# An encoder block on one core: one hand-written TensorE order, single stores for branch B's tiles, paired weight halves on GpSimd, and gate steps moved ahead of the last transpositions

## The chip, the cores and the metric

The kernel runs on one core of a Trainium2 chip. Inside the core, TensorE multiplies matrices, VectorE and ScalarE work on whole tiles, GpSimd does some of the element-wise work, and SyncE (SP in the profile) issues the transfers between the device's memory and the on-chip memory. [...] TensorE's results land in a memory of their own, PSUM.

The metric is the device time of one execution in microseconds (us).

## The reference

The kernel computes one encoder block on 1024 tokens of width 1024, with 16 learned meta tokens put in front (1040 rows):

```python
h = concatenate([meta_tokens, x])
n = rms_norm(h, norm_mix)
qa, ka, va, qb, kb, vb, ga, gb = split(n @ w_in)
y_a = differential_attention(qa, ka, va)   # 4 heads, all 1040 keys, two softmaxes each
y_b = windowed_gqa(qb, kb, vb, sink)       # 8 heads, 2 key groups, keys within 128 tokens and the meta tokens
merged = sigmoid(ga) * (y_a @ w_branch_a) + sigmoid(gb) * (y_b @ w_branch_b)
h = h + merged @ w_out
h = h + (silu(m @ w_ff_gate) * (m @ w_ff_up)) @ w_ff_down     # m = rms_norm(h, norm_ffn)
out = rms_norm(h, norm_final)[16:]
```

All products are made in float32 quality: each operand is split into a high half and a low half, and TensorE adds three products of halves (high by high, high by low, low by high).

## The kernel before

The work on TensorE has five stretches, one after the other.

**Projections and branch B (to about 295 us).** The normalised tokens lie transposed in `hT_hi` and `hT_lo`. `project_steps` multiplies them by 128 columns of `w_in` at a time; results go through a stage buffer (`qk_stage`, `va_stage`) and out to the device's memory (`qa_d`, `ka_d`, `va_d`; stores at lines 649, 657, 659, 666). Between these products run branch B's tiles: `attend_b(g, t, qb)` does the 4 heads of key group `g` for token tile `t` (scores, softmax, transposition, values), and its `finish` writes the tile's 64 x 512 result with four stores of 64 x 128 into `yb_d` (line 445). There are 16 such tiles. In this stretch the order of the instructions on each engine is set by a planner, which simulates the program with costs of its own.

**Branch A beside the gates (about 295 to 623 us).** For each of 4 heads and 8 token tiles, `scores_a` makes scores and two softmaxes, `transpose_a` turns the result through TensorE, and `values_a` multiplies by the values. The gate products (`ga` and `gb` for the same tokens) fill the gaps. They are done by a seven-product scheme over column pairs `k` and parts `p`: `order_g` lists 56 products, and `gate_steps` gives each as four steps of three matmuls (line 881), so there are 224 steps. The operand of a product is made on GpSimd by `weights_g`: sums of raw weight blocks where the part needs them (lines 780 to 793), a cast for the high half (line 799) and a subtraction for the low half (line 800). Raw weights come with the loads at line 760, at most four ahead.

Head 0's keys and queries are loaded by `load_a` (lines 943 and 945, key half m=1 first), its values by `load_v`, and one quadrant of `hT` is overwritten with mixed tokens by `turn_into(2)` (line 824). All these loads, and branch B's stores, are issued by SP in one line.

The order in this stretch is written out by hand: inside `tc.manual_schedule` an engine keeps program order. For the first token tile the program does two weight operands, `load_a`, two more, `load_v`, then `fill(G_FIRST)`, which is 24 gate steps (six products, 72 matmuls), and `turn_into(2)`. Then the tile's slots run: a character string says in which order one step each of scores (`s`), transposition of the tile before (`t`), gates (`g`) and the tail (`n`, values and norm of earlier tiles) comes. `SLOTS` is used for tiles 0 to 23 and `SLOTS_LAST`, the same string, for 24 to 32, where number 32 only finishes tile 31. A gate step is only given out while `n_gates` lasts: it starts at 224 - `HOLD` = 202, and the last 22 steps come after the loop.

Before the change, this hand-written order is cut in two. The first manual stretch covers TensorE and GpSimd and ends after `turn_into(2)`; a second one, for TensorE alone, begins there. Within each piece the order is kept; how the two pieces mix at the seam is the planner's.

**Merging the branches (623 to 710 us), output projection (to about 804 us), FFN (to the end).** `yb_d` is read back for the merge at line 1142. These stretches are not touched by the change.

Helpers that the rows name: line 120 is the subtraction of `split`, line 926 the copy of far distances for a tile (`far_copy`), line 995 the copy of the meta keys' weights that the third transposition of a tile needs, line 994 the combination of the two softmaxes, lines 980 and 984 the scores' bias and minimum on VectorE, line 887 and line 894 copies of gate results out of PSUM.

Of the kernel before, what the change touches and what calls it, by code (L numbers as in the profile page):

```python
# [9 lines left out]
F32 = mybir.dt.float32  # L10
# [4 lines left out]
ALU = mybir.AluOpType  # L15
# [4 lines left out]
P = 128  # L20
S = 1024
# [5 lines left out]
NT = S // P  # L27
# [11 lines left out]
PP2 = 2  # L39
COMBINE_POOL = (0, 1, 2, 3)  # L40
SLOTS = "ssgsgntssgsgntgnt"
SLOTS_LAST = "ssgsgntssgsgntgnt"
S_BUFS = (2, 2)
AT_BUFS = 2
G_BUFS = 3
# [29 lines left out]
def encoder_block(ctx: ExitStack, tc: tile.TileContext, x, meta, norm_mix, w_in, lq1, lk1, lq2, lk2,  # L75
# [7 lines left out]
    def f32(ap):  # L83
        return ap.bitcast(F32)
# [20 lines left out]
    t_d = [dram.tile([P, 2, 4, 512], F32, name=f"t_d{i}") for i in range(4)]  # L105
    u_d = [dram.tile([P, 512], F32, name=f"u_d{i}") for i in range(8)]
    ya_d = [dram.tile([P, S], F32, name=f"ya_d{h}") for h in range(4)]
    yb_d = [dram.tile([P, S], F32, name=f"yb_d{h}") for h in range(4)]

    ident = const.tile([P, P], F32, name="ident")  # L110
    make_identity(nc, ident)
# [270 lines left out]
    def attend_b(g, t, qb):  # L382
        nm = f"{g}_{t}"
        b0, b1 = max(t - 1, 0), min(t + 2, NT)
        nb = b1 - b0
        W = nb * 144
        j0 = b0 - t + 1
        tb = tbx[:, j0:j0 + nb, :].rearrange("p j k -> p (j k)")
        st = bpool.tile([P, 4, 432], F32, tag="bs", name=f"bs_{nm}", bufs=2)
        mn = small.tile([P, 4], F32, tag="bmn", name=f"bmn_{nm}")  # L390
        dn = small.tile([P, 4], F32, tag="bdn", name=f"bdn_{nm}")
        es = small.tile([P, 4], F32, tag="bes", name=f"bes_{nm}")
        hs = slice(4 * g, 4 * g + 4)
        for r in range(4):
            ps = bank(psum1, "bs", f"bps_{nm}_{r}", 2)
            for v in range(2):
                nc.tensor.matmul(ps[:, :W], qb[:, r, t * P:(t + 1) * P],  # L397
                                 kb[g][:, v, b0:b1, :].rearrange("p b k -> p (b k)"), start=(v == 0), stop=(v == 1))
            nc.vector.tensor_tensor_reduce(st[:, r, :W], ps[:, :W], tb, 2.0 ** -(4 * g + r + 1), nsink[:, 4 * g + r:4 * g + r + 1],  # L399
                                           ALU.add, ALU.min, mn[:, r:r + 1])  # L400
        nc.vector.tensor_tensor(es, mn, sinkb[:, hs], ALU.add)
        for r in range(4):
            nc.scalar.activation(st[:, r, :W], st[:, r, :W], AF.Exp, bias=mn[:, r:r + 1], scale=-1.0,
                                 accum_out=dn[:, r:r + 1])
        nc.scalar.activation(es, es, AF.Exp)
        nc.vector.tensor_tensor(dn, dn, es, ALU.add)
        nc.vector.reciprocal(dn, dn)  # L407
        for r in range(4):
            scaled.append(nc.gpsimd.tensor_scalar(st[:, r, :W], st[:, r, :W], dn[:, r:r + 1], 1.0, ALU.mult, ALU.mult))  # L409

        md = mds[t % 2]
        own = (t - b0) * 144 + P
        nc.gpsimd.tensor_copy(md.rearrange("p (r a k) -> p r a k", r=4, a=2),
                              st[:, :, own:own + NM].unsqueeze(2).broadcast_to([P, 4, 2, NM]))

        def finish():
            py = bank(psum1, "by", f"bpy_{nm}", 1)
            for k in [8, *range(b0, b1)]:
                o = (k - b0) * 144
                pt = bank(psum1, "bt", f"bpt_{nm}_{k}", 2).rearrange("p (r t) -> p r t", r=4)  # L420
                if k == 8:
                    nc.tensor.transpose(pt[:, 0, :], md, ident)
                    tm = tms[t % 2]
                    hi = bpool.tile([P, P], F32R, tag="bmh", name=f"bmh_{nm}", bufs=1)
                    nc.scalar.activation(hi, pt[:, 0, :], AF.Copy, scale=of_hi)
                    for r in range(4):
                        at = slice(32 * r, 32 * r + 32)
                        nc.vector.scalar_tensor_tensor(tm[at, r], pt[at, 0, :], of_x[at], f32(hi[at]), ALU.mult, ALU.subtract)
                    nc.tensor.matmul(py, vb[g][:, 8, :], tm.rearrange("p r t -> p (r t)"), start=True, stop=False)
                    continue  # L430
                for r in range(4):
                    nc.tensor.transpose(pt[:, r, :], st[:, r, o:o + P], ident)
                tr = bpool.tile([P, 2, 4, P], F32R, tag="btr", name=f"btr_{nm}_{k}", bufs=4)
                nc.scalar.activation(tr[:, 0], pt, AF.Copy)
                nc.vector.tensor_tensor(tr[:, 1], pt, f32(tr[:, 0]), ALU.subtract)
                for hl in range(2):
                    nc.tensor.matmul(py, vb[g][:, k, :], tr[:, hl].rearrange("p r t -> p (r t)"),  # L437
                                     start=False, stop=(k == b1 - 1 and hl == 1))
            y1 = bpool.tile([64, 512], F32, tag="by1", name=f"by1_{nm}", bufs=2)
            nc.scalar.copy(y1, py[64:128])  # L440
            nc.vector.tensor_tensor(y1, py[0:64], y1, ALU.add)
            for jj in range(2):
                for par in range(2):
                    r = 2 * jj + par
                    nc.sync.dma_start(yb_d[2 * g + jj][64 * par:64 * par + 64, t * P:(t + 1) * P],
                                      y1[:, r * P:(r + 1) * P])
        return finish

    qb = new_qb(0)
# [309 lines left out]
                    after.enter_context(tc.issue_after(keys_a[0].ins))  # L759
                raws_g.append(nc.sync.dma_start(w, w_in[:, col:col + P].rearrange("(c p) n -> p c n", p=P)))  # L760

    sums_g, keys_a, raws_g, values_in, turned_t = {}, [], [], [], {}

    def weights_g(n):
        k, p = order_g[n]
        load_g()
        tt = nc.gpsimd.tensor_tensor
        nm = f"{k}_{p}"
        kind = "s" if n >= n_first else "m" if p == 6 and k < 5 else "f"
        wa, wb = raw_g[kind, k, 0], raw_g.get((kind, k, 1))  # L770
        a11, a12 = wa[:, 0:4], wa[:, 4:8]
        if wb is not None:
            a21, a22 = wb[:, 0:4], wb[:, 4:8]
        if p == 1:
            src = a11
        elif p == 2:
            src = a12
            n_freed[0] += 1 if k < 5 else 2 if k < 7 else 0
        elif p == 6:
            tt(a21, a21, a22, ALU.add)  # L780
            tt(a21, a21, a11, ALU.subtract)
            src = a21
            if k < 5 or k == 7:
                n_freed[0] += 2
        elif p == 5:
            src = sums_g[k] = gwork.tile([P, 4, P], F32, tag="s", name=f"s1g_{k}", bufs=1)
            tt(src, a21, a22, ALU.add)
        elif p == 7:
            tt(a21, a11, a21, ALU.subtract)
            src = a21  # L790
        elif p == 3:
            tt(a12, a12, a11, ALU.add)
            tt(a12, a12, sums_g.pop(k), ALU.subtract)
            src = a12
        else:
            src = a22
            n_freed[0] += 2
        op = ops_g[n] = wpool.tile([P, 2, 4, P], F32R, tag=("wh", "wl")[n % 2], name=f"wopg_{nm}", bufs=W_BUFS)
        nc.gpsimd.tensor_copy(op[:, 0], src)
        tt(op[:, 1], src, f32(op[:, 0]), ALU.subtract)  # L800

    def ensure_g(n):
        while n_made[0] < min(n, len(order_g)):
# [267 lines left out]
        if t % 4 == 3:  # L1071
            yield from normed_a(h, t // 4, acc[0])

    order_pe = tc.manual_schedule(engines={mybir.EngineType.PE, mybir.EngineType.Pool})
    order_pe.__enter__()
    tiles, turning, tail = [], iter(()), []

    def step_tail():
# [3 lines left out]
    for n in range(AH * NT + T_LAG):  # L1082
# [3 lines left out]
        if n < AH * NT:  # L1086
            h, t = divmod(n, NT)
            if t == 0:
                if not h:
                    ensure_g(2)  # L1090
                ld = load_a(h)
                if not h:
                    ensure_g(4)
                load_v(h, ld[2])
                fill(G_HEAD if h else G_FIRST)
                if not h:
                    turn_into(2)
                    order_pe.__exit__(None, None, None)
                    order_pe = tc.manual_schedule(engines={mybir.EngineType.PE})
                    order_pe.__enter__()  # L1100
            if t % 2 == 0:
                at_ = apool.tile([P, 9, 2, 256], F32R, tag="at", name=f"at{h}_{t}", bufs=AT_BUFS)
            s = [None, None]
            tiles.append((h, t, s, at_, ld[2]))
            scoring = scores_a(h, t, ld, s)
        if n >= T_LAG:
            turning = turn(tiles[n - T_LAG])
        for what in SLOTS if n < 3 * NT else SLOTS_LAST:
            if what == "s":
                next(scoring, None)  # L1110
            elif what == "t":
                next(turning, None)
            elif what == "n":
                step_tail()
            else:
                fill(1)
# [22 lines left out]
        nc.sync.dma_start(raw.rearrange("p (c n) -> p c n", n=P), w_bb[:, o * P:(o + 1) * P].rearrange("(c p) n -> p c n", p=P))  # L1139
    for j in range(4):  # L1140
        for h in range(2):
            nc.sync.dma_start((a12, w11)[h][:, j], yb_d[j][:, h * 512:h * 512 + 512])
    ypool, close_ypool = pool("ypool")
    first_w = [branch_w(ypool, o, w_bb, "b", raw) for o, raw in enumerate((a11[:, 2], asum[:, 0]))]

# [725 lines left out]
```

## Time and profile before

| | us |
|---|---|
| median of 3 runs | 1429.8 (1429.32 to 1431.39) |
| the profiled execution | 1430.58 |
| its span, first to last instruction | 1428.7 |
| TensorE busy in it | 1404.2 (98%) |
| VectorE, ScalarE, GpSimd busy | 917.9, 672.7, 636.9 |

A row of the timeline gives the start in us from the span's start, the duration, the engine, the source line and the operation; in square brackets stands the idle time just before it and what ended that. "SPq" is the time in which SP issues a transfer, not the time of the transfer. Matmuls overlap in the pipeline: one is recorded with 0.39 us, while the next starts 0.23 us later, so the spacing of the starts is what one costs.

### The profile page before, as it was taken

How to read it: one execution, taken by the hardware profiler on the slowest of the kernel's cores; microseconds unless marked ns; L12 is line 12 of the kernel's file. 1: busy time of each engine (PE TensorE's matmuls, PEld its weight loads, DVE VectorE, ACT ScalarE, POOL GpSimd, SP SyncE). 2: the span in 40 equal slices, each digit the busy share in tenths (PEclk: the TensorE clock that was granted, in tenths of full speed). 3: DMA queues.
4: the chain of work that ended last, by engine and by line, in shares of the span. 5: the costliest groups of instructions: out<-in, count | busy, mean ns of one | idle time of the engine just before them, and what ended most of it. 6: DMA issues, size and time to landing. Idle time of an engine off the chain costs nothing.

```text
span 1428.7 us, 20729 instructions
## 1 busy us (share of the span) xinstructions
PE 1404.2 (98%) x7183; PEld 1205.1 (84%) x7183; DVE 917.9 (64%) x1584; ACT 672.7 (47%) x1284; POOL 636.9 (45%) x648
## 2 busy tenths in 40 slices
PE   9999999989999999999999999999999999999998
PEld 8998999978888888888888888888888888888886
DVE  6555666517777878665978966555544553787566
ACT  6355556425445555554346654333333333444454
POOL 4256865537676657232503045554454442000442
PEclk9999999999999999999999999999999999999999
DMA  8446465487796353197332724423332232954443
GB/s 230 92 127 187 138 212 158 109 271 232 235 305 229 126 186 119 38 337 223 123 143 81 207 83 145 152 100 102 111 104 96 97 110 100 357 185 142 125 127 145
DMA packets 195066, 228.28 MB, mean 160 GB/s; under 512 B 17592, under 2 KB 128128, under 8 KB 194960
## 3 DMA queue, kind: packets, MB, share of 16 engines
q1 hardware_dynamic: 193040, 224.12, 48.5%
q10 hardware_dynamic: 1920, 2.83, 0.7%
q8 instruction: 57, 0.93, 0.3%
q14 instruction: 49, 0.40, 0.1%
HBM read 152.48 MB, written 67.86 MB: 154 GB/s over the span
## 4 chain that ended last, share of the span: by engine, by line
PE 88%; DVE 6%; DMA 2%; ACT 2%; issue 1%; SPq 1%; POOL 0%; ACTq 0%; DVEq 0%; POOLq 0%
PE pg L1634 29%; PE pd L1738 15%; PE pg L881 8%; PE ppa L724 6%; PE po L1537 4%; PE pp_ka L230 3%; PE pp_va L230 3%; PE pp_qa L230 3%; PE aps L977 3%; PE apy L1019 2%; PE bps L397 2%; PE pp_qb L230 2%; PE po L1545 2%; DVE as L994 2%; DVE as L980 1%; PE bpy L437 1%
## 5 line engine op out<-in xcount | busy, mean ns | idle before, releaser
L1634 PE MATMUL pg<-t,wop 128*128 128x512 f32 x1056 | 242.4, 389 | 0.0
L1634 PEld LDWEIGHTS pg<-t,wop 128*128 128x128 f32 x1056 | 198.2, 188 | 41.2
L120 POOL TENSOR_TENSOR wop<-wf,wop 128x512 fp32r<-128x512 f32 x114 | 151.9, 1333 | 163.5 <-ACT wop L119 152.2
L1738 PE MATMUL pd<-ob,oa 128*128 128x512 f32 x924 | 209.6, 389 | 0.0
L1738 PEld LDWEIGHTS pd<-ob,oa 128*128 128x128 f32 x924 | 173.4, 188 | 36.0
L1634 PE MATMUL pg<-b,wop 128*128 128x512 f32 x792 | 183.3, 389 | 0.0
L1634 PEld LDWEIGHTS pg<-b,wop 128*128 128x128 f32 x792 | 148.4, 188 | 30.7
L881 PE MATMUL pg<-hT_hi,wopg 128*128 128x512 f32 x448 | 170.8, 403 | 0.8 <-ACT p L887 0.8
L119 ACT ACTIVATE wop<-wf 128x512 fp32r<-128x512 f32 x128 | 80.7, 632 | 73.0 <-PE pg L1634 51.5
L120 POOL TENSOR_TENSOR oa<-ra,oa 128x512 fp32r<-128x512 f32 x27 | 35.0, 1296 | 168.6 <-ACT oa L119 167.2
L988 ACT ACTIVATE as<-as,amn 128x1040 f32<-128x1040 f32 x64 | 74.6, 1165 | 52.9 <-DVE amn L984 52.8
L119 ACT ACTIVATE oa<-ra 128x512 fp32r<-128x512 f32 x77 | 48.7, 632 | 107.6 <-PE pd L1738 50.3
L977 PE MATMUL aps<-ak,aq 128*128 128x352 f32 (+1 forms) x384 | 87.0, 334 | 9.4 <-DMA ak<-ka_d 5.6
L881 PEld LDWEIGHTS pg<-hT_hi,wopg 128*128 128x128 f32 x448 | 85.1, 190 | 13.0 <-ACT p L887 1.1
L881 PE MATMUL pg<-hT_lo,wopg 128*128 128x512 f32 x224 | 88.8, 396 | 0.0
L1411 DVE TENSOR_TENSOR s<-wf,wf 128x512 f32<-128x512 f32 x22 | 16.2, 738 | 111.0 <-DMA wf<-in_w_ff_up_dram 69.4
L980 DVE CUSTOM_DVE_ANT_0 as<-aps,dist,far_a 128x704 f32<-128x704 f32 x64 | 60.3, 942 | 36.5 <-PE aps L977 36.2
L977 PEld LDWEIGHTS aps<-ak,aq 128*128 128x128 f32 x384 | 64.4, 189 | 20.4 <-DVE amn L980 6.7
L399 DVE CUSTOM_DVE_ANT_0 bs<-bps,tbx,nsink 128x432 f32<-128x432 f32 (+1 forms) x64 | 38.5, 627 | 54.9 <-PE bps L397 33.5
L1009 ACT ACTIVATE at<-apt 128x512 fp32r<-128x512 f32 (+1 forms) x96 | 45.4, 484 | 58.3 <-PE apt L1006 58.3
L409 POOL TENSOR_SCALAR bs<-bs,bdn 128x432 f32<-128x432 f32 (+1 forms) x64 | 37.2, 601 | 75.9 <-DVE bdn L407 48.9
L1019 PEld LDWEIGHTS apy<-at,av 128*128 128x128 f32 x400 | 54.2, 190 | 4.0
(321 smaller groups left out, 3137.4 us busy)
## 6 DMA issues: line engine op xcount, KB each, us to landing
ra<-aop SPq DMA_DIRECT2D x77, 256.0 KB, 2.6
wf<-in_w_ff_gate_dram SPq DMA_DIRECT2D x25, 512.0 KB, 3.6
wf<-in_w_ff_up_dram SPq DMA_DIRECT2D x25, 512.0 KB, 3.6
aop<-as SPq DMA_DIRECT2D x44, 256.0 KB, 2.1
w_c<-in_w_in_dram SPq DMA_DIRECT2D x17, 512.0 KB, 4.5
aop<-c SPq DMA_DIRECT2D x33, 256.0 KB, 2.0
ak<-ka_d SPq DMA_DIRECT2D x16, 520.0 KB, 6.1
t_d<-tst SPq DMA_DIRECT2D x16, 512.0 KB, 4.1
```

What stands on the lines that cost most here:

```text
L119: high = nc.scalar.activation(hi, src, AF.Copy)
L120: lo_eng.tensor_tensor(lo, src, f32(hi), ALU.subtract)
L230: product = nc.tensor.matmul(ps[:, :n], a[:, c, :], b[:, c, at:at + n], start=(u == 0), stop=(u == 3 * DC - 1))
L724: nc.tensor.matmul(ps, w[:, a, j, :], src(j, b, tk), start=(j == 0 and n == 0), stop=(j == 3 and n == 2))
L881: nc.tensor.matmul(ps, op[:, x, c, :], h[:, 4 * d + c, HALF[t]], start=(p in (1, 6, 7) and c == 0 and i == 0), stop=(p in (2, 6, 3, 4) and ...
L977: nc.tensor.matmul(ps[:, :n], qs[m][:, t * P:(t + 1) * P], ks[m][:, vv, k0:k0 + n], start=(vv == 0), stop=(vv == 1))
L980: nc.vector.tensor_tensor_reduce(s[m][:, 0:2 * n].rearrange("p (a k) -> p a k", a=2), two[:, :, :n], dist[:, u0:u0 + 2 * n].rearrange("p ( ...
L988: nc.scalar.activation(s[m][:, 0:L], s[m][:, 0:L], AF.Exp, bias=mn[:, m, 1:2], scale=-1.0, accum_out=dn[:, 1:2] if m else first_sum)
L1019: nc.tensor.matmul(py[:, cols], v[:kp, a, k, :], at_[:kp, k, b, :], start=(k == 0 and j == 0), stop=(k == 8))
L1537: nc.tensor.matmul(sets_o[p][u], oa[:, a, u * P:(u + 1) * P], ob[:, b, :], start=(p in (1, 5) and j == 0 and k == 0), stop=(p in (2, 3) an ...
L1634: nc.tensor.matmul(ps, op[:, x, c, :], b[:, y, c, :], start=(p in (1, 5) and c == 0 and n == 0), stop=(p in (4, 2, 3) and c == 3 and n == ...
L1738: nc.tensor.matmul(ps[u], oa[:, a, u * P:(u + 1) * P], ob[:, b, :], start=(p in (1, 2, 5) and j == 0 and k == 0), stop=(p in (2, 3, 4) and ...
```

## The change

- `SLOTS_LAST` becomes `"ggggntgntnt"` and is used only for number 32 of the loop; tiles 24 to 31 use `SLOTS`.
- `yb_d` becomes two tensors of 256 rows in place of four of 128, and a branch B tile is stored by one transfer of 64 x 4 x 128 instead of four of 64 x 128. The reading at line 1142 follows.
- In `weights_g` each operand's cast is held behind the subtraction of the operand before it, so that cast and subtraction of one operand stand as a pair on GpSimd.
- TensorE's manual stretch is no longer cut: it runs in one piece from the first gate step to the end of the loop and beyond. GpSimd has a manual stretch of its own, which ends where both ended before.

```diff
-SLOTS_LAST = "ssgsgntssgsgntgnt"
+SLOTS_LAST = "ggggntgntnt"
...
-    yb_d = [dram.tile([P, S], F32, name=f"yb_d{h}") for h in range(4)]
+    yb_d = [dram.tile([2 * P, S], F32, name=f"yb_d{h}") for h in range(2)]
...
             nc.scalar.copy(y1, py[64:128])
             nc.vector.tensor_tensor(y1, py[0:64], y1, ALU.add)
-            for jj in range(2):
-                for par in range(2):
-                    r = 2 * jj + par
-                    nc.sync.dma_start(yb_d[2 * g + jj][64 * par:64 * par + 64, t * P:(t + 1) * P],
-                                      y1[:, r * P:(r + 1) * P])
+            nc.sync.dma_start(yb_d[g][:, t * P:(t + 1) * P].rearrange("(r d) t -> d r t", r=4),
+                              y1.rearrange("d (r t) -> d r t", r=4))
         return finish
...
-        nc.gpsimd.tensor_copy(op[:, 0], src)
-        tt(op[:, 1], src, f32(op[:, 0]), ALU.subtract)
+        with ExitStack() as after:
+            if made_g:
+                after.enter_context(tc.issue_after(made_g[-1].ins))
+            nc.gpsimd.tensor_copy(op[:, 0], src)
+            made_g.append(tt(op[:, 1], src, f32(op[:, 0]), ALU.subtract))
...
-    order_pe = tc.manual_schedule(engines={mybir.EngineType.PE, mybir.EngineType.Pool})
+    order_pe = tc.manual_schedule(engines={mybir.EngineType.PE})
     order_pe.__enter__()
+    order_pool = tc.manual_schedule(engines={mybir.EngineType.Pool})
+    order_pool.__enter__()
...
                 fill(G_HEAD if h else G_FIRST)
                 if not h:
                     turn_into(2)
-                    order_pe.__exit__(None, None, None)
-                    order_pe = tc.manual_schedule(engines={mybir.EngineType.PE})
-                    order_pe.__enter__()
+                    order_pool.__exit__(None, None, None)
...
-        for what in SLOTS if n < 3 * NT else SLOTS_LAST:
+        for what in SLOTS if n < AH * NT else SLOTS_LAST:
...
-            nc.sync.dma_start((a12, w11)[h][:, j], yb_d[j][:, h * 512:h * 512 + 512])
+            nc.sync.dma_start((a12, w11)[h][:, j], yb_d[j // 2][j % 2 * P:j % 2 * P + P, h * 512:h * 512 + 512])
```

More of the change, by code (lines that the diff above doesn't have):

```diff
@@ L760, in load_g @@
                 raws_g.append(nc.sync.dma_start(w, w_in[:, col:col + P].rearrange("(c p) n -> p c n", p=P)))
-    sums_g, keys_a, raws_g, values_in, turned_t = {}, [], [], [], {}
+    sums_g, keys_a, raws_g, values_in, turned_t, made_g = {}, [], [], [], {}, []
     def weights_g(n):
```

## The prediction

> **What bounds the kernel now.** The page comes first: TensorE is busy almost throughout.
>
> ```profile
> span 1428.7 us, 20729 instructions
> PE 1404.2 (98%) x7183; PEld 1205.1 (84%) x7183; DVE 917.9 (64%) x1584; ACT 672.7 (47%) x1284; POOL 636.9 (45%) x648
> ```
>
> So only TensorE's own idle time, and any time in which it runs slowly, can be won. The view of the waits, for TensorE alone, names the idle time:
>
> ```profile
> engine line waited for: us in total, times, longest us
> PE aps L977 <- DMA ak<-ka_d: 5.6, 1, 5.6
> PE aps L977 <- DVE amn L980: 3.8, 12, 0.4
> PE apt L1006 <- DVE as L994: 1.7, 1, 1.7
> ...
> PE pg L881 <- ACT p L887: 0.8, 1, 0.8
> ```
>
> One wait of 5.6 us stands out: the first score matmuls of branch A wait for the keys of head 0. The table of stages shows where it lies, and that it costs more than itself (columns: stretch, its length, busy time and instructions of each engine, granted TensorE clock, DMA share, GB/s; the first row is of TensorE alone):
>
> ```profile
> 165.00:295.00 130.00, 130.00 (x787) 1.00 0.57 163
> 303.40:309.38 5.98, 0.40 (x2) 0.03 (x1) 0.00 (x0) 0.57 (x1) 4.24 (x5) 0.82 1.08 390
> 309.38:314.50 5.12, 5.12 (x14) 4.16 (x15) 0.00 (x0) 0.23 (x1) 0.00 (x0) 0.54 1.04 392
> ```
>
> Before 295 us TensorE has no gap. After the wait the granted clock is 0.54 for five microseconds, and the transfers run at some 390 GB/s. The timeline of TensorE gives the steps:
>
> ```profile
> 294.99 0.39 PE L881 MATMUL pg<-hT_hi,wopg 128*128 128x512 f32 x1
> ...
> 303.41 0.39 PE L881 MATMUL pg<-hT_lo,wopg 128*128 128x512 f32 x1
> 309.38 0.63 PE L977 MATMUL aps<-ak,aq 128*128 128x352 f32 x1 [5.59 <-DMA ak<-ka_d]
> ...
> 314.07 0.65 PE L977 MATMUL aps<-ak,aq 128*128 128x352 f32 x3
> 314.56 0.39 PE L881 MATMUL pg<-hT_hi,wopg 128*128 128x512 f32 x1
> ...
> 321.71 0.81 PE L977 MATMUL aps<-ak,aq 128*128 128x352 f32 x4
> 322.36 0.39 PE L881 MATMUL pg<-hT_hi,wopg 128*128 128x512 f32 x1
> ```
>
> The gate matmul at 303.41 is the 38th. The program wrote 72 ahead of the first scores, but at the seam between the two hand-written pieces the planner put one score matmul after the 38th and three after the 48th.
>
> **TensorE's order in one piece.** The scores go back behind all 72 gate matmuls; the two kernels' orders differ on TensorE nowhere else from 295 us on. A gate matmul costs (303.41 - 294.99) / 37 = 0.2276 us. By 314.56 the old order has done 48 of them and four score matmuls. Four score matmuls cost 322.36 - 321.71 = 0.65 us, so that work without wait and at full clock takes 48 x 0.2276 + 0.65 = 11.57 us and would be done at 306.56. The head of this stretch can thus give back 314.56 - 306.56 = 8.0 us: 309.38 - 303.41 - 0.23 = 5.74 us of standing still, and 2.26 us of half clock.
>
> [...]
>
> **What has to be ready earlier.** The first scores now start at 294.99 + 72 x 0.2276 = 311.38 us. SP's timeline and the keys' transfers say whether the data is there:
>
> ```profile
> 294.73 2.46 SPq L445 DMA_DIRECT2D yb_d<-by  x4
> 297.29 0.60 SPq L666 DMA_DIRECT2D va_d<-va_stage  x1
> 297.99 0.61 SPq L657 DMA_DIRECT2D ka_d<-qk_stage  x1
> ...
> 300.63 1.21 SPq L760 DMA_DIRECT2D wg_f<-in_w_in_dram  x2
> 301.88 1.22 SPq L943 DMA_DIRECT2D aq<-qa_d  x1
> 303.20 0.85 SPq L945 DMA_DIRECT2D ak<-ka_d  x2
> ...
> 304.57 1.10 SPq L945 DMA_DIRECT2D ak<-ka_d  x2
> 305.77 0.51 SPq L760 DMA_DIRECT2D wg_f<-in_w_in_dram  x1
> ```
>
> ```profile
> DMA to landing us min/median/max: 6.0/7.7/9.4
> ```
>
> Keys m=1: the second of the pair is issued at about 303.6 and with the median lands at 311.3, just in time for 311.38. Keys m=0: the last is issued at about 305.0 and with the largest value lands at 314.4. They are needed after 72 gate matmuls, four scores (0.65), six more gate matmuls (1.37) and two scores (an estimate of 0.3 from the same rows), at 313.7. That would leave a wait of 0.7 us.
>
> **Single stores for branch B.** SP is busy without a gap from 294.73 to the keys, so the last tile's stores delay them. One issue in place of four: 2.46 us become 0.6, if a transfer of 256 short rows costs SP what the row at 297.29 shows. Everything behind it, gate weights and keys, then starts 1.85 us earlier and the 0.7 us vanish. If the issue instead costs four times as much, the shift is nothing. I take 1.85; the nearest rows are all about 0.6. On TensorE this part alone is worth nothing: the row 165 to 295 is full, so the cover is TensorE's own work. It makes the planner lay out the rest of branch B anew, from the seventh tile on. That cannot win anything there; as an upper bound I take the rate of the small waits of branch A (3.8 us in 328 us, by the waits above), which for 130 us is 1.5 us. I take 0, the nearest row being the full one.
>
> **Operands on GpSimd.** The gates' 72 matmuls in one run need the fifth and sixth operand earlier:
>
> ```profile
> 304.77 0.61 POOL L799 CAST wopg<-wg_f 128x512 fp32r<-128x512 f32 x1 [5.44 <-DMA wg_f<-in_w_in_dram]
> 305.46 1.26 POOL L800 TENSOR_TENSOR wopg<-wg_f,wopg 128x512 fp32r<-128x512 f32 x1
> 306.67 0.61 POOL L799 CAST wopg<-wg_f 128x512 fp32r<-128x512 f32 x1
> ...
> 308.56 0.61 POOL L799 CAST wopg<-wg_f 128x512 fp32r<-128x512 f32 x1
> 317.54 0.62 POOL L799 CAST wopg<-wg_f 128x512 fp32r<-128x512 f32 x1 [8.36 <-PE pg L881]
> 318.11 1.30 POOL L800 TENSOR_TENSOR wopg<-wg_f,wopg 128x512 fp32r<-128x512 f32 x1
> ```
>
> The fifth operand's low half is done at 306.72 and is needed by the 51st matmul, at 306.37: 0.35 us late, or 1.5 us early with SP's shift. The seventh's cast at 308.56 got its subtraction only at 318.11, because another operand's cast stood between them and waited 8.36 us for TensorE to release a buffer. With the pairing it follows at once, done by about 310.5, and is needed after 312. The ninth operand is the next that could be late: its load goes out at 305.77, 1.85 us earlier with the shift, and with 9.4 us to land and 0.61 + 1.30 us of work plus a copy of line 926 between them (an estimate of 0.5 from the casts) it is ready at 315.7 to 317.6; two more products (24 x 0.2276) and six score groups (about 2.85) put its need at 319.7. So the pairing costs nothing here. Elsewhere it saves nothing either: no TensorE wait in the view above names GpSimd. Bounds: from 0 to the third rival's price; I take 0.
>
> **Gates ahead of the last transpositions.** This part does nothing. The 202 steps are spent sooner: 24 in front, 3 x 6 at the later heads, 2 at the second tile, and five per tile make 44 + 160 = 204 by tile 31. In number 32 every `g` and `s` finds nothing to give out, and both strings reduce to n, t, n, t, n, t. The last tile's wait on line 994, the one of 1.7 us above, stays.
>
> **Sum.** 8.0 us off and nothing put back. The profiled execution took 1430.58 us, which becomes 1422.6; it lies 0.8 above the median of 1429.8, which becomes 1421.8. If SP's shift fails (0.7) and branch B loses its bound (1.5), it is 1424.0.
>
> **Rivals.**
> First, the wait moves. The transfers run at 390 GB/s and each takes 6.0 to 9.4 us; with TensorE 8 us earlier and the loads at most 1.85, some load becomes the new last. For it speaks the ninth operand's spare time of 2 to 4 us and the keys' of 0 to 2. Against it, a single late load delays all later needs with it, so such waits do not add up. A load 2 to 4 us late gives back as much: 1424 to 1426, say 1425. [...]
>
> Second, the gain is hidden anyway: something behind the head sets the end of branch A. Against it, TensorE waits for nothing long later, and what waits there are come from TensorE's own chain, which moves with it. The time would be 1429.8.
>
> Third, the other side: the pairing slows the whole of branch A. GpSimd works in order, and a pair that waits for TensorE's release holds back the copy at line 995, on which the third transposition of every tile hangs. At 32 tiles and 0.35 us each, 11.2 us would be lost, giving 1433.0; above 0.25 us per tile it eats the gain, above 0.34 it is slower than before by over 0.2%. Against it speaks that GpSimd now waits at that copy for VectorE, not the other way (31 tiles, 314 to 600 us):
>
> ```profile
> L995 POOL COPY as<-as 128x32 f32<-128x32 f32 x31 | 6.6, 212 | 22.0 <-DVE as L994 20.8 <-DVE adn L991 1.2
> ```
>
> **How the numbers follow.** The forecast has 0.72, with its own range of 1420.3 to 1423.8. The moved wait has 0.13, the hidden gain 0.07, the slower branch A 0.08. About 0.2% (2.9 us) is what a measurement can tell. Forecast and moved wait are both faster: 0.85; same 0.07; slower 0.08. The range from 1420.2 to 1424.8 holds the forecast and some two thirds of the moved wait.
>
> **What would show it.** Right: no wait on `ak<-ka_d`, a granted clock of 1.00 throughout 295 to 321 us, 72 gate matmuls in a row, the scores of tile 0, m=0 at about 313.7 instead of 321.71, branch A's end 8 us earlier, SP's store issues for a tile at about 0.6. Wrong: a new wait of TensorE between 303 and 325 us on a load or on GpSimd, idle time before 295 us, or many short waits of line 1006 on line 995.

## The result, and the profile after

The changed kernel takes 1424.4 us (median of 6 runs, 1423.2 to 1426.1) against 1429.6 us for the kernel before (6 runs beside it, 1428.3 to 1431.4). The ratio is 0.9963, with a 95% interval of 0.9950 to 0.9975: faster, by 5.2 us. The prediction was 1421.8 us within 1420.2 to 1424.8. The sign and the range held; the likeliest value was 2.6 us too low.

The page of the changed kernel answers the first fence of the prediction; the profiled execution took 1424.24 us.

```profile
span 1421.9 us, 20667 instructions
PE 1401.0 (99%) x7183; PEld 1202.7 (85%) x7183; DVE 914.8 (64%) x1584; ACT 672.1 (47%) x1284; POOL 636.7 (45%) x648
```

The view of TensorE's waits for the changed kernel, over branch A's stretch (in us: total, times, longest):

```profile
PE apt L1006 <- DVE at L1010: 2.3, 4, 0.8
PE aps L977 <- DVE amn L980: 2.2, 7, 0.4
PE pg L881 <- POOL wopg L800: 1.8, 1, 1.8
PE apt L1006 <- DVE as L994: 1.7, 1, 1.7
```

The wait of 5.6 us on the keys is gone. A new one stands there: 1.8 us on GpSimd's low half of a weight operand. The timeline of TensorE places both:

```profile
293.52 0.39 PE L881 MATMUL pg<-hT_hi,wopg 128*128 128x512 f32 x1
...
309.88 0.80 PE L977 MATMUL aps<-ak,aq 128*128 128x352 f32 x4
...
312.21 0.81 PE L977 MATMUL aps<-ak,aq 128*128 128x352 f32 x4
...
338.89 0.51 PE L881 MATMUL pg<-hT_hi,wopg 128*128 128x512 f32 x1 [1.76 <-POOL wopg L800]
...
615.11 0.50 PE L721 MATMUL ppa<-yb,wbhb 128*128 128x512 f32 x1 [0.78 <-DVE g L912]
```

The 72 gate matmuls take 309.88 - 293.52 = 16.36 us, 0.227 us each, with no gap, and the scores of m=0 follow 18.69 us after the first gate matmul. The granted clock is 1.00 in all three stretches of the table of stages (columns as in the prediction):

```profile
303.00:309.50 6.50, 6.50 (x31) 5.37 (x30) 0.00 (x0) 1.17 (x2) 6.24 (x7) 1.00 1.02 406
309.50:338.50 29.00, 26.52 (x144) 22.45 (x142) 20.00 (x49) 15.37 (x28) 13.72 (x17) 1.00 0.90 311
338.50:348.00 9.50, 9.11 (x58) 8.31 (x59) 6.62 (x16) 3.26 (x7) 5.94 (x9) 1.00 0.70 211
```

The new wait has its cause in GpSimd's timeline. The operand that is late is the twelfth: the matmul behind the wait is the 135th gate matmul, the third of the twelfth product, and the cast at 335.34 below is the twelfth. (The expectations further down call this operand the eleventh.)

```profile
328.82 1.29 POOL L777 TENSOR_TENSOR wg_f<-wg_f 128x512 f32<-128x512 f32 x1 [4.80 <-DMA wg_f<-in_w_in_dram]
330.06 0.21 POOL L995 COPY as<-as 128x32 f32<-128x32 f32 x1
330.22 1.30 POOL L778 TENSOR_TENSOR wg_f<-wg_f,wg_f 128x512 f32<-128x512 f32 x1
334.12 1.28 POOL L777 TENSOR_TENSOR wg_m<-wg_m 128x512 f32<-128x512 f32 x1 [2.59 <-DMA wg_m<-in_w_in_dram]
335.34 0.61 POOL L799 CAST wopg<-wg_f 128x512 fp32r<-128x512 f32 x1
...
336.31 1.29 POOL L778 TENSOR_TENSOR wg_m<-wg_m,wg_m 128x512 f32<-128x512 f32 x1
337.55 1.28 POOL L800 TENSOR_TENSOR wopg<-wg_f,wopg 128x512 fp32r<-128x512 f32 x1
```

Its sum is finished at 331.5. But then GpSimd stands for 2.59 us at the sum of another operand (`wg_m`), whose raw weights have not landed; the cast follows at 335.34, and the other operand's second sum at 336.31 comes between the cast and the subtraction at 337.55. TensorE resumes as that one ends.

A measure that leaves the stretches before and after aside is the time from the first gate matmul to the first matmul of the branch merge. Before it was 622.82 - 294.99 = 327.83 us (the merge's row stands here, from the timeline of the kernel before); in the changed kernel it is 615.11 - 293.52 = 321.59, which is 6.24 us less.

```profile
622.82 0.50 PE L724 MATMUL ppa<-yb,wbhb 128*128 128x512 f32 x1 [0.78 <-DVE g L912]
```

Over all the traces of this study the gates start anywhere between 292.7 and 295.0 us. The kernel of sums_behind and sums_again, one and the same, gave 292.71 and 293.69, so a start that differs by 1 us tells nothing. "Length of branch A" is this measure in what follows.

### The profile page after: what moved, and what is told of

It is laid out like the page before. It is cut to its first block, busy times and chain, and to the rows that moved or that the text cites. A ratio compares the mean times of both kernels' runs of the same rounds, so it can differ in the third digit from the quotient of the medians.

```text
span 1421.9 us, 20667 instructions
## 1 busy us (share of the span) xinstructions
PE 1401.0 (99%) x7183; PEld 1202.7 (85%) x7183; DVE 914.8 (64%) x1584; ACT 672.1 (47%) x1284; POOL 636.7 (45%) x648
## 4 chain that ended last, share of the span: by engine, by line
PE 90%; DVE 4%; DMA 2%; ACT 1%; issue 1%; SPq 1%; POOL 1%; ACTq 0%; POOLq 0%; DVEq 0%
PE pg L1634 29%; PE pd L1738 14%; PE pg L881 8%; PE ppa L721 6%; PE po L1537 4%; PE pp_va L230 3%; PE pp_ka L230 3%; PE aps L977 3%; PE pp_qa L230 3%; PE apy L1019 3%; PE pp_qb L230 3%; PE bps L397 2%; PE po L1545 2%; PE bpy L437 1%; PE apt L1006 1%; PE bpt L432 1%
```

## The experiments

The question was which part carries the gain. Theory, by the prediction: the one piece on TensorE alone. Rival: the wait moves unless the other parts are there. Each ratio is to the kernel before, run beside the experiment.

### Each part alone, and all but one

**seam_only.** The kernel before, with TensorE's order in one piece and nothing else:

```diff
-    order_pe = tc.manual_schedule(engines={mybir.EngineType.PE, mybir.EngineType.Pool})
+    order_pe = tc.manual_schedule(engines={mybir.EngineType.PE})
     order_pe.__enter__()
+    order_pool = tc.manual_schedule(engines={mybir.EngineType.Pool})
+    order_pool.__enter__()
...
-                    order_pe.__exit__(None, None, None)
-                    order_pe = tc.manual_schedule(engines={mybir.EngineType.PE})
-                    order_pe.__enter__()
+                    order_pool.__exit__(None, None, None)
```

> The kernel before with one part of the change: TensorE's hand-written order in one piece, GpSimd's ending where it did. My theory: this part is the gain. All 72 gate matmuls stand ahead of the first scores, no wait on the keys m=1, no half clock. Branch B's stores still hold up SP, so the keys of m=0 come about 0.7 us late and the fifth operand's low half 0.35, and the eleventh operand's low half, behind another operand's sums on GpSimd, some 1 to 2 us late: about 1424 us, 5 to 6 less than before. Rival: without SP's earlier loads the wait only moves, and TensorE stands for 3 us or more between 303 and 320 us, with half clock after it: 1427 us or more.

Measured: 1429.5 us, ratio 1.0000 (0.9991 to 1.0009). The part on which the forecast put all of its 8.0 us wins nothing alone; the expectation of about 1424 failed and its rival held. The waits, the timeline of TensorE and that of GpSimd of this run, in three fences:

```profile
PE pg L881 <- POOL wopg L800: 6.2, 2, 5.9
```

```profile
317.27 0.80 PE L881 MATMUL pg<-hT_hi,wopg 128*128 128x512 f32 x1 [5.90 <-POOL wopg L800]
```

```profile
307.00 0.61 POOL L799 CAST wopg<-wg_f 128x512 fp32r<-128x512 f32 x1
315.38 0.61 POOL L799 CAST wopg<-wg_f 128x512 fp32r<-128x512 f32 x1 [7.77 <-DMA wg_f<-in_w_in_dram]
315.95 1.26 POOL L800 TENSOR_TENSOR wopg<-wg_f,wopg 128x512 fp32r<-128x512 f32 x1
```

The keys' wait is gone and one of the same size is back, 8 us later: the seventh operand's cast is done at 307.6, its subtraction starts at 315.95, because the ninth operand's cast stands between them and waits 7.77 us for its load. The half clock came along: the granted clock was 0.51 from 316.3 to 323.2.

**no_pairing.** The changed kernel without the pairing; TensorE's order is that of the changed kernel.

```diff
-        with ExitStack() as after:
-            if made_g:
-                after.enter_context(tc.issue_after(made_g[-1].ins))
-            nc.gpsimd.tensor_copy(op[:, 0], src)
-            made_g.append(tt(op[:, 1], src, f32(op[:, 0]), ALU.subtract))
+        nc.gpsimd.tensor_copy(op[:, 0], src)
+        tt(op[:, 1], src, f32(op[:, 0]), ALU.subtract)
```

> The changed kernel without the pairing of casts and subtractions; TensorE's order is the same instruction for instruction. In this GpSimd order the eleventh operand's subtraction stands behind another operand's first sum, a copy and a cast, but no longer behind its second sum. My theory: the wait of 1.8 us on GpSimd shrinks to 0.3 to 1 us, the time is 1423 to 1424.2, so the pairing gains nothing. Rival, the pairing is needed for the earlier scores: some other gate matmul waits for its low half behind a cast that waits for TensorE, 1 us or more, and the time is above 1425.5.

Measured: 1427.8 us, ratio 0.9988 (0.9979 to 0.9996). The expectation that the pairing gains nothing failed. It is the same stall as in seam_only, and what the cast waits for is its load, not TensorE as the rival had it. The timelines of TensorE and GpSimd of this run show it:

```profile
315.47 0.80 PE L878 MATMUL pg<-hT_hi,wopg 128*128 128x512 f32 x1 [4.46 <-POOL wopg L797]
```

```profile
305.35 0.61 POOL L796 CAST wopg<-wg_f 128x512 fp32r<-128x512 f32 x1
313.58 0.61 POOL L796 CAST wopg<-wg_f 128x512 fp32r<-128x512 f32 x1 [7.62 <-DMA wg_f<-in_w_in_dram]
314.15 1.26 POOL L797 TENSOR_TENSOR wopg<-wg_f,wopg 128x512 fp32r<-128x512 f32 x1
```

So the pairing is not free of effect: with the other parts in place it is worth some 3.4 us.

**cut_again.** The changed kernel with TensorE's order cut in two where it was before:

```diff
-    order_pe = tc.manual_schedule(engines={mybir.EngineType.PE})
+    order_pe = tc.manual_schedule(engines={mybir.EngineType.PE, mybir.EngineType.Pool})
     order_pe.__enter__()
-    order_pool = tc.manual_schedule(engines={mybir.EngineType.Pool})
-    order_pool.__enter__()
...
-                    order_pool.__exit__(None, None, None)
+                    order_pe.__exit__(None, None, None)
+                    order_pe = tc.manual_schedule(engines={mybir.EngineType.PE})
+                    order_pe.__enter__()
```

> The changed kernel with TensorE's order cut in two again (single stores and paired halves stay). The planner then puts the first score matmul after the 36th gate matmul. The keys are issued some 1.9 us sooner than before and TensorE arrives 0.45 us sooner, so the wait should be about 4.2 us instead of 5.6. If a wait of that length still brings the half clock, the gain over the kernel before is about 1.4 us (1428.1); if it does not, about 3.7 us (1425.9). If the single stores were the gain and not the seam, it would be as fast as the changed kernel, 1424.4.

Measured: 1427.4 us, ratio 0.9983 (0.9974 to 0.9992). TensorE waits for the keys again, 4.64 us, and behind the wait the gate matmuls start 0.43 us apart (306.50, 306.93) instead of 0.227:

```profile
306.07 0.63 PE L977 MATMUL aps<-ak,aq 128*128 128x352 f32 x1 [4.64 <-DMA ak<-ka_d]
```

The seam is needed too, then.

**stores_only** and **pairing_only.** The kernel before with the single stores (the diff's lines on `yb_d`), and with the pairing (its lines in `weights_g`).

> The kernel before with single stores, nothing else; the planner puts the first score matmul after the 36th gate matmul. Theory: as with the order cut again, the wait on the keys shrinks from 5.6 to about 4.6 us and the half clock stays: about 1428, 1 to 2.5 us less than before. If the difference between this and the cut order with pairing is under 1 us, the pairing is worth nothing where TensorE's order is cut.

> The kernel before with casts and subtractions paired, nothing else; TensorE's order is that of the kernel before. Theory: in the old order TensorE stands for the keys, and the seventh operand is not what it waits for, so the pairing alone gives nothing: 1429.6 us within 1, with the wait of 5.6 us on the keys in the trace. Rival: pairing helps by itself all through branch A: 1427 or less.

Measured: 1427.8 us, ratio 0.9991 (0.9982 to 1.0000), and 1430.5 us, ratio 1.0006 (0.9997 to 1.0015). Both keep the seam's wait on the keys, 5.0 and 5.9 us in the view of the waits. Neither part moves the time by what the measurement can tell.

**no_single_stores.** The changed kernel with the four stores per tile of before.

```diff
-            nc.sync.dma_start(yb_d[g][:, t * P:(t + 1) * P].rearrange("(r d) t -> d r t", r=4),
-                              y1.rearrange("d (r t) -> d r t", r=4))
+            for jj in range(2):
+                for par in range(2):
+                    r = 2 * jj + par
+                    nc.sync.dma_start(yb_d[2 * g + jj][64 * par:64 * par + 64, t * P:(t + 1) * P],
+                                      y1[:, r * P:(r + 1) * P])
```

> The changed kernel with four stores per tile again. Theory: SP issues the gate weights and keys some 1.9 us later, so the fifth operand's low half costs TensorE 0.35 us, the keys of m=0 about 0.7 us, and the eleventh operand, whose wait hangs on loads, stays at 1.5 to 2.5 us, measured from TensorE's earlier start: 1425 to 1426.5 us. Rival: the loads have time to spare and the stores are worth nothing: 1424.4.

Measured: 1430.1 us, ratio 1.0006 (0.9997 to 1.0014). This was a miss: the four stores were to cost 0.7 us at the keys and cost all of the gain. The waits of TensorE show the 0.7, and beside it something larger:

```profile
PE apt L1009 <- DVE at L1013: 6.7, 5, 4.6
...
PE aps L980 <- DMA ak<-ka_d: 0.8, 1, 0.8
```

The 4.6 us end at 328.94, ahead of a transposition. Followed back, VectorE (line 1013) waits for a ScalarE copy (line 1012), and that one stands in ScalarE's line behind a copy of a gate result, which waits for a stage buffer. ScalarE's and SP's timelines of this run:

```profile
326.99 0.58 ACT L897 COPY g<-pg 128x512 f32<-128x512 f32 x1 [9.18 <-DMA g_d<-g]
327.47 0.60 ACT L1012 ACTIVATE at<-apt 128x512 fp32r<-128x512 f32 x1
```

```profile
313.61 1.86 SPq L827 DMA_DIRECT2D hT_hi<-t_d  x1
315.51 1.00 SPq L827 DMA_DIRECT2D hT_lo<-t_d  x1
317.70 1.83 SPq L848 DMA_DIRECT2D g_d<-g  x2
```

In the changed kernel SP issues the first gate result's store ahead of those two loads, which read 1 MB each:

```profile
311.24 0.38 SPq L845 DMA_DIRECT2D g_d<-g  x1
...
313.87 0.36 SPq L824 DMA_DIRECT2D hT_hi<-t_d  x1
316.56 0.36 SPq L824 DMA_DIRECT2D hT_lo<-t_d  x1
```

Nothing in the change's text says so; the planner placed the store differently once branch B had fewer stores.

**store_first** tests that: no_single_stores, with the two loads held behind that one store. The order on the four compute engines is not touched.

```diff
-                        after.enter_context(tc.issue_after(raws_g[5].ins))
+                        after.enter_context(tc.issue_after(raws_g[5].ins)), after.enter_context(tc.issue_after(stored_g[2].ins))
...
-                        nc.sync.dma_start(*held_stores.pop(0))
+                        stored_g.append(nc.sync.dma_start(*held_stores.pop(0)))
```

> The four-store kernel with seam and pairing (1430.06 us), with one change: the two loads of line 827 (hT) are held behind the first store of a gate result (g_d), as SP issued them in the changed kernel. The order of the instructions on TensorE, VectorE, ScalarE and GpSimd stays as it was; on SP only that one store moves ahead of the two loads. Theory: the 4.6 us wait of TensorE came from the stage buffer whose store was issued behind these loads. Then the 9.18 us of idle time ahead of ScalarE's copy at line 897 shrinks below 5, the 4.6 us wait and its half clock go (some 6 us), the eleventh operand's wait of about 1.8 us comes back, and the keys' 0.8 us stays: 1425 to 1426. Rival: the transfers run at their limit, so the store lands as late as before or the loads behind it become the new last: a wait of 3 us or more stays between 325 and 340 us and the time stays at 1428 to 1430.

Measured: 1425.2 us, ratio 0.9970 (0.9959 to 0.9980). ScalarE's timeline, and SP's:

```profile
322.60 0.59 ACT L897 COPY g<-pg 128x512 f32<-128x512 f32 x1 [3.54 <-DMA g_d<-g]
```

```profile
314.87 1.82 SPq L848 DMA_DIRECT2D g_d<-g  x1
316.78 0.42 SPq L827 DMA_DIRECT2D hT_hi<-t_d  x1
```

The order of one store and two loads on SP is worth 4.9 us here (1430.1 to 1425.2), and no wait of TensorE between 300 and 345 us is longer than 0.9 us. The expectation was off in one point: the wait of 1.8 us on the twelfth operand did not come back. TensorE waits only 0.3 us for a low half, one product earlier.

### The last wait

**sums_behind.** The changed kernel, with the sums of an operand (lines 777 to 790) also held behind the subtraction of the operand before it, so that GpSimd makes one operand after the other:

```diff
+        hold = ExitStack()
+        if made_g:
+            hold.enter_context(tc.issue_after(made_g[-1].ins))
...
-        with ExitStack() as after:
-            if made_g:
-                after.enter_context(tc.issue_after(made_g[-1].ins))
-            nc.gpsimd.tensor_copy(op[:, 0], src)
-            made_g.append(tt(op[:, 1], src, f32(op[:, 0]), ALU.subtract))
+        nc.gpsimd.tensor_copy(op[:, 0], src)
+        made_g.append(tt(op[:, 1], src, f32(op[:, 0]), ALU.subtract))
+        hold.close()
```

> The changed kernel, with an operand's sums held behind the subtraction of the operand before too, not only its cast; TensorE's order is the same. My theory: the wait of 1.8 us in the changed kernel comes from another operand's two sums, the first of which waits for its own load, standing ahead of the eleventh operand's cast and subtraction. With the sums behind, the eleventh is ready about 4 us earlier, the wait is gone, and the time is 1.8 us less: 1422.6. Rival: the eleventh operand's own load is what is late; then the wait stays at 1.5 to 1.8 us and the time at 1424.4.

Measured: 1420.5 us, ratio 0.9935 (0.9922 to 0.9949). GpSimd's timeline of this run:

```profile
329.21 1.31 POOL L781 TENSOR_TENSOR wg_f<-wg_f,wg_f 128x512 f32<-128x512 f32 x1
330.58 0.61 POOL L799 CAST wopg<-wg_f 128x512 fp32r<-128x512 f32 x1
...
331.55 1.29 POOL L800 TENSOR_TENSOR wopg<-wg_f,wopg 128x512 fp32r<-128x512 f32 x1
```

Cast and subtraction now follow the operand's own sum, and the wait on `wopg` is gone from the view. This kernel beats both. It is also 2.1 us below what was expected (1422.6), more than the wait of 1.76 us can give; **sums_again** ran it once more in another set.

> The kernel of the run sums_behind once more: the changed kernel with an operand's sums also held behind the subtraction of the operand before. If the gain over the changed kernel is one of the kernel and not of that set of runs: 1419.5 to 1421.5, a ratio to the kernel before of 0.9925 to 0.9945, and no wait on wopg in its trace. If it was luck: 1423 to 1425.

Measured: 1421.0 us, ratio 0.9941 (0.9928 to 0.9955). The gain over the changed kernel, some 3 to 4 us, is the kernel's own. Branch A took 319.44 and 318.06 us in the two traces, 2.15 and 3.53 less than in the changed kernel. What goes beyond the 1.76 us lies in small waits, which the view of the waits adds up to 9.7 and 8.1 us in these two traces of one kernel (10.6 in the changed kernel's, with the 1.8); it was not taken apart.

**four_stores_sums.** The kernel of store_first with the same hold on the sums.

> The kernel of the run store_first, with an operand's sums held behind the subtraction of the operand before it as well. Theory: the single stores matter only through SP's order; with that order set, the four stores cost the keys' 0.8 us and no more, so this is within 1.5 us of the run sums_behind (1420.5): 1420.5 to 1422. Rival: the single stores are worth more through the transfers themselves (fewer issues, everything 1.2 to 1.9 us earlier): 1423 or more, with some wait on a load between 300 and 340 us.

Measured: 1423.7 us, ratio 0.9957 (0.9945 to 0.9970), 2.7 us above sums_again in the same set. Neither side was quite right: there is no wait on a load above 0.3 us, as the rival wanted, and the time is 1.7 us above the theory's upper end. The waits that the view lists for branch A add up to 11.0 us against 8.1 in sums_again, none of them new and large. That the single stores are worth these small waits, beyond SP's order at that one place, is argued and not shown: sums_behind, the same kernel as sums_again, lists 9.7 us.

### The slot string

**string_back.** The changed kernel with the old string; the instructions stand in the same order on every engine.

```diff
-SLOTS_LAST = "ggggntgntnt"
+SLOTS_LAST = "ssgsgntssgsgntgnt"
```

> The changed kernel with the old slot string and its old use (from tile 24 on). The instructions of every engine come out in the same order as in the changed kernel, since no gate step is left to give out in number 32. Theory: the string does nothing, and the run is a repetition of the changed kernel, 1424.4 us within 1.5. Rival: none for the order; a difference above 2 us would measure the noise between builds.

Measured: 1424.3 us, ratio 0.9965 (0.9952 to 0.9977), against 0.9963 for the changed kernel. The string does nothing. Its trace shows something else. TensorE's timeline, and the table of stages:

```profile
338.46 0.51 PE L881 MATMUL pg<-hT_hi,wopg 128*128 128x512 f32 x1 [2.15 <-POOL wopg L800]
```

```profile
339.70:343.20 3.50, 3.50 (x16) 3.21 (x16) 1.21 (x2) 0.60 (x1) 2.09 (x3) 0.51 0.84 257
```

The twelfth operand's wait is 2.15 us instead of 1.76, and this time half clock came after it (0.51 over the 3.50 us above). Branch A took 323.59 us, 2.0 more than in the changed kernel's trace, with the same instructions in the same order.

## Why the prediction was right, and where it was not

All kernels of the three parts side by side (length of branch A worked out as above from each trace):

| one piece on TensorE | single stores | pairing | ratio to before | branch A, us |
|---|---|---|---|---|
| no | no | no | 1 | 327.83 |
| yes | no | no | 1.0000 | 329.03 |
| no | yes | no | 0.9991 | 327.84 |
| no | no | yes | 1.0006 | 328.59 |
| yes | yes | no | 0.9988 | 327.19 |
| no | yes | yes | 0.9983 | 326.03 |
| yes | no | yes | 1.0006 | 327.82 |
| yes | yes | yes | 0.9963 | 321.59 |

Wherever a part is missing, TensorE waits for about 4.5 us or more at one place. Behind that wait the granted clock was 0.54 in the kernel before and 0.51 in seam_only, and in cut_again, no_pairing and no_single_stores the gate matmuls start 0.43 us apart instead of 0.227; of stores_only and pairing_only only the mean granted clock of the profiled execution is known, 0.996 and 0.997 against 0.998 for the changed kernel. Without the pairing or without the one piece, a third to a half of the gain stays (0.9988 and 0.9983); the whole of it comes only with all three.

**TensorE's order in one piece, 8.0 us off.** Right in size: the two marks set for it, 72 matmuls in a row and the scores of m=0 18.7 us after the start, came out at 16.36 and 18.69 us, with a granted clock of 1.00 from 295 to 321 us. Branch A is shorter by 6.24 us, which is the 8.0 less the new wait of 1.76. The smaller waits changed places and nearly cancel: the scores' minimum from 3.8 to 2.2 us, the transpositions' copies (line 1010) from 0.9 to 2.3. This agrees with the 2.26 us that the prediction put down for the half clock, as what was left of the 8.0 beside the standing still. It speaks weakly, because two traces of one kernel, sums_behind and sums_again, differ by 1.4 us in this measure; that 6.24 is met to the last digit is chance.

**"Nothing put back".** This is the step that failed, and the one that makes the likeliest value too low. The prediction checked the seventh operand and named the ninth as the next that could be late; the ninth was in time (its subtraction ended 23.0 us after the first gate matmul; the forecast had 20.7 to 22.6, and the need at 24.7). The twelfth was late, by 1.76 us, and not through its own load but through another operand's sums ahead of it, which the pairing does not order. So the first rival came true at a place it had not named, and its time (1424 to 1426) holds the measurement. sums_behind shows the cause: without those sums in between the wait is gone, and the kernel lands at 1420.5, below the forecast.

The rest of the 2.6 us lies in the executions. The profiled one is 6.34 us faster than the profiled one before, the medians differ by 5.2. Most of this lies with the kernel before: its profiled execution took 1.0 us more than the median of its six runs, while the changed kernel's lay 0.1 below its own. The forecast had taken over the whole 8.0 us from the profile to the median. Half clock behind the new wait, as in string_back's trace (0.51 over 3.50 us), explains little: three of the six executions of the changed kernel have a mean granted clock of 0.999, as all five of sums_again have, whose trace shows 1.00 in every stretch from 293 to 614 us, and they took 1423.2, 1424.3 and 1424.5 us.

That the stated range held was in part luck. The result lies outside the forecast's own range of 1420.3 to 1423.8, and inside the stated one only because that was stretched over part of the first rival, which got 0.13.

**"The pairing costs nothing, elsewhere it saves nothing".** The first half held; the third rival, a slower branch A, did not appear. The second half failed: the view of before named no wait on GpSimd because TensorE then stood at the keys. The prediction had seen the seventh operand's cast without its subtraction, and priced the pairing by the waits of before instead of by those that the seam's repair would uncover. Without the pairing 4.5 us came back there.

**"On TensorE the single stores are worth nothing by themselves", 0.7 us at the keys.** The sentence held literally (stores_only), and the 0.7 was measured as 0.8 (no_single_stores) and 0.6 (store_first). As a price for losing that part it was wrong by a factor of eight (5.7 us): the part also changed where the planner put one store on SP, and that store frees a stage buffer on which ScalarE, then VectorE, then TensorE hang. The prediction compared TensorE's order of the two kernels and priced SP by issue times; the place of the gate results' stores on SP was not looked at. Its case for a failing shift, 1424.0, would have read 1430.1.

**The slot string, nothing.** Right, by instruction order and by time.

The sign was therefore right for a reason that was half the reason. The 8.0 us are TensorE's, but two parts that the forecast held for nearly worthless are what kept them from being spent at the next two places.

## What to carry to other kernels

When one wait on the critical path is removed in a stretch that is crowded with transfers, list everything that was late in its shadow, one by one: here a subtraction behind another operand's cast, a store behind two loads, a cast behind another operand's sum, each of which held TensorE for 2 to 6 us once it was last. A part that is worth nothing alone can be worth the whole change together with the others, so the price of leaving it out must be worked out with the other parts in place. And compare the order on the queue that issues the transfers as closely as the order on the busiest engine: one store ahead of two loads was worth 4.9 us.

## What the runs showed of the hardware

In the kernel before, the granted clock was 0.50 from 307.22 to 314.05 us, of which 2.16 us lie inside the wait on the keys (5.59 us, to 309.38); it was 1.00 from 295.00 to 307.20 and from 314.10 to 622.00. In seam_only it was 0.51 from 316.3 to 323.2 us, around the end (317.27) of a wait of 5.90 us. In string_back it was 0.51 from 339.7 to 343.2 us, behind a wait of 2.15 us; in the changed kernel it was 1.00 over branch A, with a wait of 1.76 us at the same operand. With the same order of instructions the wait of 1.76 us went with 321.59 us for branch A, and the wait of 2.15 us with 323.59. Whether the length of a wait decides if half clock follows, or something else does, is not shown.

On SP, a store of 64 x 4 x 128 in the changed kernel cost as much to issue as one of 64 x 128 in the kernel before (medians of 0.58 and 0.59 us), so four in one saved three quarters of the issue time.
